# A two-sequence encoder: the sample's second output projection is moved from the kernel's last stage to the end of the stage before

## The chip, the core and the metric

The kernel runs on one core of a Trainium2 chip. The core has a matrix engine (PE, with its weight loads shown apart as PEld), three engines for elementwise work (DVE, ACT, POOL) and a queue that issues DMA transfers (SP, shown as SPq). Each engine works through its own instructions in the order in which they stand. The metric is the device time of one execution in microseconds; lower is better.

## The reference

Two sequences go through the same two-layer encoder with the same weights: the prompt (2048 tokens, called Q or `p` in the kernel) and the sample (1024 tokens, called S or `s`). Width is 1024. One layer is:

```python
xn = rms_norm(h, norm_g)
proj = xn @ w_in
ya = block_attention(qa, ka, va) * silu(a_gate)          # softmax attention over the own tokens
yb = rms_norm(gated_delta_rule(both directions)) * ...   # a scan over chunks of 64 tokens
yc = rms_norm(gla_chunked(both directions)) * ...        # a second, lighter scan
ym = block_attention(m_q, km, vm) * silu(m_gate)         # attention over 256 memory tokens
h = h + concatenate([ya, yb, yc, ym]) @ w_out
```

After two layers `y = rms_norm(h, final_norm_g)`. The mixers `ya`, `yb`, `yc`, `ym` have 4 heads of 64 columns each, so each gives 256 of the 1024 columns that `w_out` reads. All is float32.

## The kernel before

Every projection is a product of 128-wide tiles in which both operands are split into a high and a low part (`whi`, `wlo`, `xhi`, `xlo`); line 280 (`mm3`) issues three matmuls for each of 8 slices of the contraction. An output projection of 512 tokens is 384 such matmuls of 256 columns. Attention (lines 586 to 657) goes by units of one head and 512 query tokens. A unit first takes maxima (line 586, DVE line 587: 16 matmuls for 2048 keys), then for 16 tiles of 128 keys it computes scores (lines 656 and 657), an exponential (`p`, ACT), the product with the values (line 643) and a running sum of `p` on POOL (`acc`, line 155); line 614 sums that over the partitions, and a store to `yT` ends the unit. The prompt's layer has 16 units on memory tokens and then 16 main units; between the 8th and the 9th main unit the keys and values (`kst`, `kh`, `vst`, one buffer each) are loaded anew. The chunk scan (lines 930 to 963, called the scan here) does 32 steps for the prompt, one per 128 tokens and direction. Line 1064 and after are the lighter scan (gla), line 881 the norm of either.

Work is written as streams (Python generators) that `merge` interleaves by estimated costs, and a scheduler then orders each engine's instructions with priorities. One stream, `right`, holds the scans and the sample's mixers through the whole program. Beside it the program runs one stage after the other:

- `projP1`: the prompt's first output projection and second projection (`outproj(Q, 0)`, `proj(Q, 1)`), with the sample's second-layer mixers and the preparation of the prompt's scan in `right`
- slot 3: the prompt's second-layer attention (`mixaP`) and gla (`glaP`) beside what is left in `right`, which is the prompt's scan; it ends when gla and `right` are done
- the last stage: `out_final`, beside what is left of the attention. It goes by blocks of 512 tokens: two of the sample, then four of the prompt. Each block loads the mixers' output (`h<-syT`, `h<-pyT`), splits it, multiplies by four column groups of `w_out`, adds `h` in a tile `ht` and takes the final norm there (`norm_rows`, line 539). Block b of the prompt may start when 10 + 2b main units are done.

The function `outproj`, used for the first layer, goes by blocks of up to 1024 tokens: it adds the residual and stores `h` to DRAM. Projection tiles (pools `xp`, `wp`, `sp`) are freed at the end of a projection stage, and slot 3's tiles take their place.

Of the kernel before, what the change touches and what calls it, by code (L numbers as in the profile page):

```python
# [16 lines left out]
P = 128  # L17
D = 1024
# [5 lines left out]
HB = 3  # L24
# [48 lines left out]
class Kern:  # L73
# [436 lines left out]
    def out_final(self, X, L, hp):  # L510
        nc, I = self.nc, self.I
        g = self.rep(hp, "grep", I["final_norm_g"], D)
        for blk in range(0, X.S, 512):
            n = X.S // 512
            yield from until(lambda: X.mixed >= {("d", L), ("l", L)} and (("a", L) in X.mixed or X.units_done >= 6 * n + 2 * (blk // 512 + 1)))
            xs = self.x_tiles(512)
            ht = self.t(hp, [P, 4, D], "ht", bufs=2)
            self.ld(ht, X.h[blk:blk + 512].rearrange("(j p) c -> p j c", p=P))
            first = self.load_w("wout", (L, 0), 256)()
            yield from self.y_block(X, blk, xs)  # L520

            def sink(c):
                def f(b, ps):
                    v = ht[:, b // P:b // P + 2, c * 256:c * 256 + 256]
                    self.vtt(v, ps, v, ALU.add)
                    if c == 3:
                        for j in (b // P, b // P + 1):
                            self.norm_rows(ht[:, j], g)
                            self.st(X.y[blk + j * P:blk + (j + 1) * P], ht[:, j])
                return f  # L530
            yield from self.groups([("wout", (L, c), 256) for c in range(4)], first, xs, lambda c, w, halves: self.gemm_tok(w, xs, halves, sink(c)))

    def norm_rows(self, h, grep):
        n = h.shape[0]
        junk = self.t(self.sp, [P, D], "gt", mybir.dt.bfloat16)[0:n]
        ss = self.t(self.sp, [P, 1], "ss")[0:n]
        self.act(junk, h, AF.Square, accum_out=ss)
        y = self.rstd(self.sp, ss, 1, 1.0 / D, "xr")
        self.nc.vector.scalar_tensor_tensor(out=h, in0=h, scalar=y, in1=grep, op0=ALU.mult, op1=ALU.mult)
# [578 lines left out]
    def run(self, S, Q):  # L1118
        self.kmT = [self.dram(f"kmT{L}", (256, 512)) for L in range(2)]
        self.vm = [self.dram(f"vm{L}", (512, 256)) for L in range(2)]  # L1120
        go = lambda *streams: merge(self, streams, [right])
        beside = lambda name, *gens: go(Stream(name, chain(*gens)))

        def flow():
            for L in range(2):
                yield from self.gdn(S, L)
                if L:
                    yield from until(lambda: self.slot >= GATE)
                yield from self.gla(S, L, "right", "d")
                yield from self.mixa(S, L, "right", "d")  # L1130
                if L:
                    yield from until(lambda: self.slot >= GATE)
                yield from self.gdn(Q, L)

        def mixes(L):
            return (Stream("mixaP", self.mixa(Q, L, "left", "a")), Stream("glaP", self.gla(Q, L, "left", "l")),
                    Stream("wait", until(lambda: ("d", L) in Q.mixed)))

        right = Stream("right", flow())
        self.slot = 0  # L1140
        self.beside_proj()
        self.open_proj(1024)
        beside("projS0", self.memkv(0), self.memkv(1), self.proj(S, 0))
        beside("projP0", self.proj(Q, 0))
        beside("projS1", self.outproj(S, 0), self.proj(S, 1))
        self.close_proj()
        self.slot = 1
        self.three_mixes()
        go(*mixes(0))
        self.slot = 2  # L1150
        self.beside_proj()
        self.open_proj(1024)
        beside("projP1", self.outproj(Q, 0), self.proj(Q, 1))
        self.close_proj()
        self.slot = 3
        self.three_mixes()
        attn, gla, wait = mixes(1)
        merge(self, [attn, gla, wait], [right], lambda: gla.done and right.done)
        self.beside_out(attn.done)
        self.open_proj(512, "right")  # L1160
        with self.tc.tile_pool(name=self.nm("hp"), bufs=1, side="right") as hp:
            merge(self, [Stream("out", chain(*(self.out_final(X, 1, hp) for X in (S, Q))))], [attn])
        self.close_proj()


# [16 lines left out]
def merge(k, main, side, stop=None):  # L1182
    streams = [*main, *side]
    k.finished.clear()
    for s in streams:
        s.t = 0.0
    stop = stop or (lambda: all(s.done for s in main))
    while not stop():
        live = [s for s in streams if not s.done]
        s = min(live, key=lambda z: z.t)  # L1190
        cost = s.step(k)
        if cost is None:
            s.t = min(o.t for o in live if o is not s) + 500
        else:
            s.t += cost * k.pace.get(s.name, 1)


def until(ready):
    while not ready():
        yield None  # L1200


def chain(*gens):
    for g in gens:
        yield from g
# [65 lines left out]
```

## Time and profile before

| what | value |
|---|---|
| median of 3 runs | 5354.94 us (5354.33 to 5359.36) |
| profiled execution, its own time | 5357.58 us |
| its span, first to last instruction | 5355.5 us |
| PE busy | 4720.6 us, 88% of the span |
| DVE, ACT, POOL busy | 59%, 43%, 35% |
| mean granted clock of PE | 0.941 of full speed |

A busy share of PE is the union of the modelled durations of its matmuls. A window's difference between its length and PE's busy time is called PE's idle time here. Matmuls overlap in the pipeline, so the durations of single rows add up to more than the busy time.

### The profile page before, as it was taken

The numbers are of one execution on the slowest core, as the hardware profiler recorded it, in microseconds if no ns is written. First come the engines' busy times: TensorE is split into PE (matmuls) and PEld (weight loads), VectorE is DVE, ScalarE is ACT, GpSimd is POOL, SyncE is SP. The second block draws the span as 40 slices with busy tenths as digits, with TensorE's granted clock in tenths as the row PEclk, the third lists the DMA queues.
The fourth block names the chain that finished last, engine by engine and source line by source line (L and its number), as shares of the span: only waits on it lengthen the run. The fifth ranks groups of instructions, "written<-read, shape, count | busy, mean of one in ns | idle before, by whom it ended". The sixth has DMA issues, their size and how long they took to land. (4 is left out here: it accounts for less than half of the span.)

```text
span 5355.5 us, 76432 instructions
## 1 busy us (share of the span) xinstructions
PE 4720.6 (88%) x26984; PEld 3644.7 (68%) x26984; DVE 3158.9 (59%) x6175; ACT 2278.8 (43%) x5027; POOL 1864.0 (35%) x1836
## 2 busy tenths in 40 slices
PE   6888999999868887578889889998888989989998
PEld 5777888777757787434455468666777866545887
DVE  4375244454567664588866665636626578877553
ACT  4363233333453534454444432425326365544322
POOL 0141112023332432287656320334215335656212
PEclk8998999999879999789899999999999999999999
DMA  5475353442675743242222246326536542231774
GB/s 192 163 232 182 115 167 120 143 137 94 193 229 179 230 144 91 78 109 58 77 62 70 71 166 216 124 81 187 183 117 200 154 116 79 63 102 42 257 268 151
DMA packets 530118, 755.99 MB, mean 141 GB/s; under 512 B 196096, under 2 KB 389382, under 8 KB 494408
## 3 DMA queue, kind: packets, MB, share of 16 engines
q1 hardware_dynamic: 529736, 751.11, 44.0%
q8 instruction: 214, 3.51, 0.3%
q14 instruction: 168, 1.38, 0.1%
HBM read 490.41 MB, written 260.51 MB: 140 GB/s over the span
## 5 line engine op out<-in xcount | busy, mean ns | idle before, releaser
L280 PE MATMUL b<-whi,xhi 128*128 128x256 f32 x3520 | 1012.2, 288 | 45.7 <-ACT whi L149 13.5
L280 PE MATMUL b<-wlo,xhi 128*128 128x256 f32 x3520 | 1012.0, 288 | 0.5 <-DVE wlo L152 0.5
L280 PE MATMUL b<-whi,xlo 128*128 128x256 f32 x3520 | 1008.0, 288 | 1.1 <-DVE xlo L152 1.1
L155 POOL TENSOR_TENSOR acc<-acc,p 128x512 f32<-128x512 f32 x544 | 741.0, 1362 | 380.0 <-ACT p L146 345.0
L280 PEld LDWEIGHTS b<-whi,xhi 128*128 128x128 f32 x3520 | 681.2, 194 | 75.8 <-ACT xhi L149 24.8
L280 PEld LDWEIGHTS b<-wlo,xhi 128*128 128x128 f32 x3520 | 681.2, 194 | 29.1 <-issue 22.4
L280 PEld LDWEIGHTS b<-whi,xlo 128*128 128x128 f32 x3520 | 679.3, 193 | 30.9 <-issue 22.5
L587 DVE TENSOR_REDUCE mx<-b 128x1 f32<-128x512 f32 (+1 forms) x832 | 502.6, 622 | 322.7 <-PE b L586 318.8
L280 PE MATMUL b<-xhi,whi 128*128 128x512 f32 x1472 | 590.5, 402 | 34.6 <-ACT stg L149 28.8
L146 ACT ACTIVATE p<-b 128x512 f32<-128x512 f32 x736 | 416.9, 595 | 463.2 <-PE b L657 446.0
L280 PE MATMUL b<-xlo,whi 128*128 128x512 f32 x1472 | 588.4, 400 | 0.6 <-DVE xlo L152 0.6
L280 PE MATMUL b<-xhi,wlo 128*128 128x512 f32 x1472 | 587.8, 400 | 0.0
L656 PE MATMUL b<-qh,kst 128*128 128x512 f32 x736 | 344.5, 470 | 41.9 <-DVE mx L587 37.5
L643 PE MATMUL b<-p,vst 128*64 128x512 f32 x1280 | 358.3, 630 | 5.3 <-ACT p L146 4.2
L586 PE MATMUL b<-kst,qh 128*128 128x512 f32 (+1 forms) x832 | 340.2, 436 | 24.6 <-ACT p L146 10.8
L280 PEld LDWEIGHTS b<-xhi,whi 128*128 128x128 f32 x1472 | 276.7, 188 | 114.7 <-ACT stg L149 32.7
L280 PEld LDWEIGHTS b<-xlo,whi 128*128 128x128 f32 x1472 | 276.0, 187 | 73.4 <-issue 9.0
L280 PEld LDWEIGHTS b<-xhi,wlo 128*128 128x128 f32 x1472 | 275.4, 187 | 70.0 <-issue 5.3
L657 PE MATMUL b<-qlm,kh 68*128 68x512 f32 x736 | 297.2, 417 | 14.5 <-DVE qlm L152 14.2
L149 ACT ACTIVATE stg<-b 128x512 f32<-128x512 f32 (+3 forms) x218 | 115.5, 541 | 422.9 <-PE b L280 329.0
L656 PEld LDWEIGHTS b<-qh,kst 128*128 128x128 f32 x736 | 142.3, 194 | 217.6 <-DVE mx L587 104.9
L586 PEld LDWEIGHTS b<-kst,qh 128*128 128x128 f32 x832 | 157.3, 196 | 152.7 <-ACT p L146 49.3
(248 smaller groups left out, 9094.9 us busy)
## 6 DMA issues: line engine op xcount, KB each, us to landing
wlo<-lo_wg SPq DMA_DIRECT2D x48, 1024.0 KB, 7.4
whi<-hi_wg SPq DMA_DIRECT2D x48, 1024.0 KB, 7.2
pcmb<-cm SPq DMA_DIRECT2D x32, 1028.0 KB, 5.5
cm<-pcmb SPq DMA_DIRECT2D x64, 514.0 KB, 3.6
whi<-hi_wout SPq DMA_DIRECT2D x28, 1024.0 KB, 8.5
wlo<-lo_wout SPq DMA_DIRECT2D x28, 1024.0 KB, 6.3
h<-in_wg_dram SPq DMA_DIRECT2D x48, 512.0 KB, 8.2
hi_wg<-whi SPq DMA_DIRECT2D x24, 1024.0 KB, 9.4
```

Source lines behind the costliest of these rows:

```text
L146: self.nc.scalar.activation(out=out, in_=in_, func=func, **k)
L149: self.nc.scalar.activation(out=out, in_=in_, func=AF.Copy)
L155: self.nc.gpsimd.tensor_tensor(out=out, in0=a, in1=b, op=op)
L280: self.nc.tensor.matmul(out=out, lhsT=a, rhs=b, start=(i == 0), stop=(i == len(terms) - 1))
L586: nc.tensor.matmul(out=ps, lhsT=qh[:, qt * P:(qt + 1) * P], rhs=kst[:, lb * LB:(lb + 1) * LB])
L587: nc.vector.tensor_reduce(out=mx[:, qt, lb:lb + 1], in_=ps, axis=AX.X, op=ALU.max)
L643: return nc.tensor.matmul(out=pv[r], lhsT=vst[:, lt, 0:64], rhs=p, start=(lt < 2), stop=(lt >= NL - 2))
L656: nc.tensor.matmul(out=s, lhsT=kst[:, lt * P:(lt + 1) * P], rhs=qh, start=True, stop=False)
L657: nc.tensor.matmul(out=s, lhsT=kh1[0:68, lt * P:(lt + 1) * P], rhs=qlm[0:68], start=False, stop=True)
```

## The change

The sample's second-layer output projection is taken out of the last stage. It now stands behind `proj(Q, 1)` in the stage `projP1`, done by `outproj` as one block of 1024 tokens, which stores `h` to DRAM. A new function `final_norm` follows it: for each of 8 tiles of 128 tokens it loads `h`, takes the norm and stores the result. The last stage keeps the prompt's four blocks.

```diff
+    def final_norm(self, X):
+        g = self.rep(self.sp, "grep", self.I["final_norm_g"], D)
+        for t in range(0, X.S, P):
+            h = self.t(self.sp, [P, D], "h", bufs=HB)
+            self.ld(h, X.h[t:t + P])
+            self.norm_rows(h, g)
+            self.st(X.y[t:t + P], h)
+            yield 1500
...
-        beside("projP1", self.outproj(Q, 0), self.proj(Q, 1))
+        beside("projP1", self.outproj(Q, 0), self.proj(Q, 1), self.outproj(S, 1), self.final_norm(S))
...
-            merge(self, [Stream("out", chain(*(self.out_final(X, 1, hp) for X in (S, Q))))], [attn])
+            merge(self, [Stream("out", self.out_final(Q, 1, hp))], [attn])
```

Lines behind 532 have a number higher by 9 in the changed kernel. The order of instructions is the same on every engine up to the last projection of `projP1`, and differs from there on.

The first place is PE at the end of `projP1`, where the last matmuls of `proj(Q, 1)` stand (`whi_37515` and `wlo_37516` are its last weights). Before, the scan's first steps follow them at once, and shortly behind this piece come the attention's first maxima (L586):

```order
L280 MATMUL b_7255_38224<-whi_37515,xhi_5492_27394 128x256
L280 MATMUL b_7255_38224<-wlo_37516,xhi_5492_27394 128x256
L280 MATMUL b_7255_38224<-whi_37515,xlo_5493_27395 128x256
L938 MATMUL b_7189_37629<-kvi_37608,xtb_7170_37576 128x128 x4
L950 MATMUL b_7191_37639<-ka_37609,wbd_7172_37578 128x128 x4
L962 MATMUL b_7194_37698<-ubd_7174_37580,ka_37609 128x128
L930 MATMUL b_7201_37731<-kvi_37722,xtb_7171_37577 128x128 x4
L963 MATMUL b_7194_37698<-sbd_7176_37582,gq_37638 128x128
L962 MATMUL b_7194_37698<-ubd_7174_37580,ka_37609 128x128
L963 MATMUL b_7194_37698<-sbd_7176_37582,gq_37638 128x128
L934 MATMUL b_7202_37737<-sy_37730,nbd_7181_37587 128x128 x4
```

Now matmuls of the sample's output projection (`whi_38348`, `wlo_38349` are a part of `w_out`) stand there, and the scan's steps between them (L943 is L934 of before):

```order
L280 MATMUL b_7284_38410<-whi_38348,xhi_5490_27392 128x256
L280 MATMUL b_7284_38410<-wlo_38349,xhi_5490_27392 128x256
L943 MATMUL b_7188_37623<-sy_37616,nbd_7180_37586 128x128 x4
L280 MATMUL b_7284_38410<-whi_38348,xlo_5491_27393 128x256
L280 MATMUL b_7284_38410<-whi_38348,xhi_5490_27392 128x256
L280 MATMUL b_7284_38410<-wlo_38349,xhi_5490_27392 128x256
```

768 matmuls of L280 are moved ahead in this way, and 10 of the scan's 32 steps stand among them.

The second place is PE between the 8th and the 9th main unit of the attention, where the keys change: line 614 ends unit 8, line 586 begins unit 9. Before, a step of the scan stands there:

```order
L963 MATMUL b_8419_42239<-sbd_7178_37584,gq_42141 128x128
L614 MATMUL b_9029_44500<-acc_44157,c_ones 64x256
L962 MATMUL b_8420_42247<-ubd_7175_37581,ka_42112 128x128
L963 MATMUL b_8420_42247<-sbd_7179_37585,gq_42141 128x128
L962 MATMUL b_8420_42247<-ubd_7175_37581,ka_42112 128x128
L963 MATMUL b_8420_42247<-sbd_7179_37585,gq_42141 128x128
L586 MATMUL b_9042_44553<-kst_9031_44512,qh_44548 128x512
```

Now only the attention's own instructions stand there (L652 is L643 of before, L623 is L614, L595 is L586):

```order
L652 MATMUL b_9090_45160<-p_45260,vst_8143_42141 64x512
L623 MATMUL b_9126_45276<-acc_45161,c_ones 64x256 x2
L595 MATMUL b_9139_45329<-kst_9128_45288,qh_45324 128x512
L595 MATMUL b_9140_45332<-kst_9128_45288,qh_45324 128x512
L595 MATMUL b_9141_45335<-kst_9128_45288,qh_45324 128x512
```

The scan and gla have ended by then: their last instructions on PE stand at the end of unit 7, where before gla ended at unit 7 and the scan at unit 12 of 16. From unit 8 to most of unit 11 nothing but attention stands on PE; then the prompt's first output block begins. Up to unit 7 the mix is much as before: between the ends of units 1 and 7 stand 8 steps of the scan (before 9), 15 of gla (before 14) and 26 transposed norms (before 24).

The third place is SP at the start of slot 3, where gla's first loads stand (`up`, `bias`, `low`). Before:

```order
L137 DMA pgl<-stg_38273 128x2x256
L137 DMA q_7318_38500<-pmqT 64x512
L137 DMA xtb_7171_37577<-pxt 32x4x32 x4
L137 DMA up_38390<-in_gla_w_gate_up_dram 16x2x128
L137 DMA bias_38392<-in_gla_b_dram 128x2
L137 DMA low_38403<-psmT 16x512
L137 DMA lq_38405<-plqkT 128x512
L137 DMA cm_38006<-pcmb 128x1028
```

Now they stand behind the last store of the new norm pass (`out_dram<-h_40170`):

```order
L137 DMA xtb_7170_37576<-pxt 32x4x32 x4
L137 DMA out_dram<-h_40170 128x1024
L137 DMA q_7765_40910<-pmqT 64x512
L137 DMA cm_39948<-pcmb 128x1028
L137 DMA q_7765_40910<-pmqT 64x512
L137 DMA up_40232<-in_gla_w_gate_up_dram 16x2x128
L137 DMA bias_40234<-in_gla_b_dram 128x2
L137 DMA nbd_7181_37587<-pcmb 32x4x32 x2
L137 DMA low_40245<-psmT 16x512
```

Eight such stores stand in this stretch of SP now and none before, and each waits on SP until its norm is done.

## Rows read from the trace of the kernel before

**Rows 1.** The profile's page: its first line.

```profile
span 5355.5 us, 76432 instructions
```

**Rows 2.** Windows: stretch, its length, busy us (and instructions) by engine, clock, DMA.

```profile
4226.00:4310.00 84.00, 66.92 (x433) 56.26 (x432) 45.61 (x97) 42.56 (x101) 39.06 (x59) 0.92 0.53 142
4310.00:4510.00 200.00, 190.72 (x1057) 130.79 (x1055) 161.42 (x314) 119.50 (x276) 83.14 (x87) 1.00 0.35 99
4510.00:4774.00 264.00, 240.99 (x1192) 141.86 (x1193) 221.17 (x439) 126.84 (x317) 155.62 (x139) 0.98 0.21 61
4774.00:4966.00 192.00, 176.83 (x829) 102.86 (x827) 131.19 (x248) 91.67 (x203) 119.80 (x105) 0.95 0.27 80
4966.00:5245.00 279.00, 277.16 (x1999) 241.13 (x1999) 136.95 (x227) 82.84 (x169) 62.37 (x43) 1.00 0.72 268
5245.00:5355.00 110.00, 87.21 (x615) 76.29 (x613) 32.86 (x65) 27.73 (x62) 19.21 (x15) 0.90 0.37 137
...
4226.00:5355.00 1129.00, 1039.82 (x6115) 749.19 (x6113) 729.21 (x1388) 491.15 (x1126) 479.19 (x448) 0.97 0.41 136
```

**Rows 3.** Groups by line and shape, PE, 4226 to 5355 us: count, busy, mean.

```profile
L280 PE MATMUL b<-whi,xhi 128*128 128x256 f32 x795 | 226.2, 286 | 9.5 <-ACT xhi L149 9.3
```

**Rows 4.** Timeline of PE at 4200 us: start, duration, row.

```profile
4200.10 0.28 PE L280 MATMUL b<-whi,xhi 128*128 128x256 f32 x1
4200.22 0.28 PE L280 MATMUL b<-wlo,xhi 128*128 128x256 f32 x1
```

**Rows 5.** Windows: `outproj(Q, 0)` beside gla; `proj(Q, 1)` beside the scan's preparation.

```profile
3125.00:3275.00 150.00, 149.09 (x1114) 132.67 (x1113) 88.91 (x185) 44.31 (x114) 26.23 (x24) 1.00 0.56 183
3650.00:3800.00 150.00, 121.63 (x624) 102.14 (x625) 95.19 (x180) 81.97 (x167) 69.46 (x74) 0.93 0.59 177
```

**Rows 6.** Waits of PE, 3640 to 3800 us: total, times, longest.

```profile
PE b L805 <- DVE qk L152: 21.8, 4, 7.4
```

**Rows 7.** Timeline of PE, attention's rows: end of unit 7, then between units 8 and 9.

```profile
4774.29 0.65 PE L614 MATMUL b<-acc,c_ones 128*64 128x256 f32 x2
...
4795.43 1.08 PE L643 MATMUL b<-p,vst 128*64 128x512 f32 x4 [0.91 <-ACT p L146]
...
4812.27 0.95 PE L586 MATMUL b<-kst,qh 128*128 128x512 f32 x3
4814.84 0.50 PE L586 MATMUL b<-kst,qh 128*128 128x512 f32 x1 [1.61 <-DVE mx L587]
4816.02 8.32 PE L586 MATMUL b<-kst,qh 128*128 128x512 f32 x12 [0.29 <-DVE mx L587]
4825.07 0.80 PE L656 MATMUL b<-qh,kst 128*128 128x512 f32 x1 [0.31 <-DVE mx L587]
```

**Rows 8.** Window of that gap, all engines.

```profile
4796.00:4825.00 29.00, 21.40 (x68) 12.39 (x64) 24.78 (x49) 10.26 (x26) 9.62 (x9) 0.68 0.45 114
```

**Rows 9.** Timeline of PE at the change from main unit 12 to 13.

```profile
4956.37 0.50 PE L656 MATMUL b<-qh,kst 128*128 128x512 f32 x1 [0.99 <-DVE mx L587]
...
4958.19 0.39 PE L597 MATMUL b<-c_identr,nm 128*4 128x512 f32 x1 [0.32 <-DVE nm L595]
...
4959.68 0.50 PE L657 MATMUL b<-qlm,kh 68*128 68x512 f32 x1 [0.52 <-DVE qlm L152]
```

**Rows 10.** Timeline of PE, end of the first layer's 16th main unit.

```profile
3015.07 1.12 PE L614 MATMUL b<-acc,c_ones 128*64 128x256 f32 x2 [6.26 <-POOL acc L155]
```

**Rows 11.** Timeline before the last output block: SP's store and load, ACT's first split.

```profile
5288.11 0.47 SPq L137 DMA_DIRECT2D pyT<-gt  x1
...
5294.94 1.15 ACT L149 ACTIVATE xhi<-h 128x512 fp32r<-128x512 f32 x2 [7.57 <-DMA h<-pyT]
```

**Rows 12.** Groups of ACT and DVE in the last stage: the final norm's two large passes.

```profile
L146 ACT ACTIVATE gt<-ht 128x1024 bf16<-128x1024 f32 x24 | 25.1, 1048 | 92.4 <-DVE ht L152 92.4
...
L539 DVE SCALAR_TENSOR_TENSOR ht<-ht,xry,grep 128x1024 f32<-128x1024 f32 x24 | 31.3, 1323 | 0.1
```

**Rows 13.** DMA issues of the last stage: KB each, median us from issue to landing.

```profile
out_dram<-ht SPq DMA_DIRECT2D x24, 512.0 KB, 5.7
```

## The prediction

> **What bounds the kernel now.** I read the page's head first: the span is 5355.5 us [rows 1], and the profiled execution took 5357.58 us, 2.1 more than its span and 2.6 more than the median of the runs, 5354.94. The sum below is made against 5357.6; I take the 2.6 off at the end.
>
> The orders agree up to the last projection of `projP1`, which in the trace is at about 4226 us, so only 4226 to 5355 us can change. I cut this tail by windows [rows 2]: the start of slot 3 (4226 to 4310), the memory units and unit 1 (to 4510), units 2 to 7 (to 4774, where the sum of unit 7 stands [rows 7]), units 8 to 12 with the rest of the scan (to 4966), the output blocks beside the last attention (to 5245), and the end. In each the reader should compare the length with PE's busy time. The differences are 17.1, 9.3, 23.0, 15.2, 1.8 and 22.8 us, together 89 of 1129: PE is busy 92% of the tail, and no other engine over 65% of it. DVE comes closest in units 2 to 7, with 221 of 264 us, 84%. So PE bounds the tail, and its idle time is all that there is to win.
>
> **The change part by part.** The change adds no matmul and takes none away. It moves 768 of them (two of six output blocks of 384), at one start every 0.12 us [rows 4] that is 92 us, and it spreads scan and attention anew. The count of rows in the tail shows that this is a third of the output work: 795 of `whi,xhi` [rows 3], and as many of each of the two other kinds, are 2385, six times 384 and a few that still belong to `proj(Q, 1)`. What the same matmuls cost I take as equal at either place, so the time changes by the idle time after, less the 89 of before. I go through it in the new order.
>
> (a) *Sample's output projection with 10 steps of the scan between.* The nearest stretch is `outproj(Q, 0)` beside gla, the same function at full width beside a recurrent mixer: 0.9 us idle in 150 [rows 5]. The other bound is `proj(Q, 1)` beside the scan's preparation: 28.4 us idle in 150 [rows 5], of which 21.8 are four waits for DVE's `qk` [rows 6], a tile that this stretch doesn't make. I take 3, bounds 1 to 28. The splits and stores of `w_out` and the residual's loads move here too; they ran under the matmuls in both places, and without that cover the last block shows the price of one exposed load and split, 6.8 us [rows 11].
>
> (b) *Start of slot 3.* It has 17.1 us idle now. What is new is `final_norm`. A tile takes a load, a square of 1.05 us, small steps, a scaling pass of 1.3 us [rows 12] and a store that lands after 5.7 us [rows 13]; only three `h` buffers turn over. Projection tiles are freed after it, and on SP gla's first loads stand behind its last store. The cover is the scan and the memory units, which stand ahead of gla on PE. The DVE and ACT passes, 8 times 1.3 and 8 times 1.05, come on engines busy 54% and 51% there [rows 2]. I take 22. Lower bound 10, if the scan that is already running fills the start; upper bound 46: the last five tiles in two rounds of about 14.5 us each (load as long as the store, passes, store), 29 us, laid bare.
>
> (c) *Memory units to unit 7.* In the order, units 1 to 7 stand among the same mix of scan, gla and norms as before, at the place where DVE is at 84%. The mix, not the length of the scan, sets the pace of this stretch. Hence I take its 9.3 + 23.0 = 32 idle us again and add 2 for the two norms more, 34; bounds 25 to 50.
>
> (d) *Units 8 to 10 alone.* Here the cover goes. Between units 8 and 9 the new keys are loaded, split and scanned for maxima: from the end of the last product of unit 8 (4795.4 + 1.1) to the first scores of unit 9 at 4825.1 are 28.6 us [rows 7], and only 16 maxima matmuls in it are the attention's (busy 0.95 + 0.50 + 8.32 = 9.8). Now the scan fills the rest, so that PE is busy 21.4 of 29 us [rows 8]. After the change the scan has ended by unit 7, and 28.6 - 9.8 = 19 us stay empty. Each change of unit shows 0.99 + 0.32 + 0.52 = 1.8 us of short waits [rows 9]; with nothing to fill them three cost 5.5. Sum 25, where before units 8 to 12 had 15.2. Bounds 12 (loads and splits come faster without the scan on SP and DVE) to 40.
>
> At this gap PE's granted clock is 0.68 over 29 us [rows 8], so that about two thirds of it lie at 1.2 of the two levels 1.2 and 2.4 GHz, though the scan is at work. The Trainium skill (TensorE: Matmul & The Clock Gate, Part 1) says that an idle array falls to the low level and gets the high one back only after it has been busy again. That speaks against the change, since an emptier gap would send unit 9 off at the low level; if 6 us of its work took 12, the forecast would be 5390. The trace agrees on the fall; no run here shows the emptier gap.
>
> (e) *Four prompt blocks beside units 11 to 16.* Now 1.8 us idle in 279. After, each next block waits for two more units, so three times some 67 attention rows stand alone between matmuls of blocks. They cover the store to `yT`, the load and the split of a new block. I take 6, three ends of unit at 1.8; bounds 2 to 25 (three times the 6.8 of rows 11).
>
> (f) *The end.* 22.8 now: the wait for unit 16, its store, the load and the split, then the norm behind the last matmul. Unit 16 now has matmuls of the third prompt block between its last tiles; after the change its last six tiles stand alone. Its sum then waits for POOL, as at the end of the first layer, 6.3 us [rows 10]. I take 28, bounds 23 to 35.
>
> Sum: 3 + 22 + 34 + 25 + 6 + 28 = 118, less 89 gives +29 us: 5357.6 + 29 - 2.6 = 5384 us. In words: the scan goes under a projection that was already dense, and the output blocks that could have filled the attention's gaps are spent when the gaps come.
>
> **The rivals.** *The idle time only moves.* The keys' gap shortens and the start hides in the scan: 1 + 17 + 30 + 18 + 4 + 24 = 94, +5, 5360 us. For it speaks that PE's busy time is conserved; against it, that the scan must be gone from the gap.
>
> *Slot 3 shrinks by the scan (faster).* If it is the scan's serial chain, and not the mix, that paces slot 3, taking 10 of 32 steps out shortens it with its idle time: (9.3 + 23.0 + 15.2) x 22/32 = 33 for (c) and (d) together, 10 for the start, 3 + 4 + 23 for the others: 73, -16, 5339 us. For it: 84 us of slot 3's start have 17 idle while the scan alone runs. Against it: PE is 91% and DVE 84% busy in units 2 to 7. It decides for faster once (c) and (d) together fall under 38.
>
> *PE waits for the scan among the projection's matmuls.* (a) at 28, the others as summed: 143, +54, 5409 us. Against it, 0.9 idle beside gla.
>
> *The norm pass holds slot 3 back.* (b) at 46: 142, +53, 5408 us. Against it, the scan and 16 memory units stand ready.
>
> **How the numbers follow.** A change of 0.2%, 10.7 us, is about what a measurement of this kernel can tell from none; so faster is under 5344, slower over 5366. My forecast holds 0.45, with a range of its own of 5366 to 5408; the moved idle time 0.20; the shrunk slot 0.15; the two waits 0.10 each. Slower has 0.45 + 0.20 = 0.65, same 0.20, faster 0.15. The range reaches down to 5342, which leaves about two thirds of the faster case out, and up to 5420, past both waits, for two bounds that meet: 0.8 within.
>
> **What would show it.** In the profile after: `L280` rows and scan rows mixed from 4226 to about 4380 with PE near 100%; unit 7 ending later than now by the 92 us moved ahead, 10 us of idle time and the last quarter of the scan; then about 19 us of empty PE beside 16 maxima matmuls, with no scan row; the first prompt block only in unit 11; units 11 to 16 beside 1536 projection matmuls; and a span near 5387. The forecast is wrong if PE's idle time behind unit 7 is under 45 us (25 + 6 + 28 = 59 is expected) or that before it under 48 (3 + 22 + 34 = 59); if the start of slot 3 has over 35 us idle, the norm pass is the cause.

## The result, and the profile after

| what | before | after |
|---|---|---|
| median | 5354.64 us (4 runs, 5349.59 to 5359.36) | 5402.05 us (4 runs, 5401.57 to 5402.85) |
| ratio | 1 | 1.0089, 95% interval 1.0071 to 1.0106 |
| span of the profiled execution | 5355.5 us | 5401.1 us |

The changed kernel is slower by about 47 us, where 29 were forecast. The windows of its tail follow, cut at the places of the terms (a) to (f): the sample's projection, the start of slot 3, the rest of it to the end of unit 7, units 8 to 10 alone, the blocks beside the attention, the end. The columns are those of [rows 2].

```profile
4226.00:4380.00 154.00, 150.64 (x1271) 149.95 (x1271) 50.09 (x95) 48.94 (x113) 34.55 (x58) 0.99 0.64 207
4380.00:4460.00 80.00, 61.10 (x390) 53.81 (x388) 50.59 (x126) 44.09 (x115) 22.32 (x37) 0.89 0.68 202
4460.00:4936.00 476.00, 431.23 (x2148) 263.86 (x2149) 408.30 (x821) 246.83 (x599) 236.00 (x218) 0.98 0.29 85
4936.00:5046.00 110.00, 92.28 (x281) 37.39 (x279) 56.00 (x84) 43.36 (x80) 65.13 (x50) 0.85 0.25 79
5046.00:5305.00 259.00, 247.06 (x1494) 181.04 (x1492) 132.71 (x196) 79.51 (x158) 102.87 (x75) 0.99 0.41 151
5305.00:5401.00 96.00, 73.74 (x514) 63.59 (x514) 32.86 (x61) 24.08 (x56) 17.03 (x13) 0.88 0.37 140
4226.00:5401.00 1175.00, 1056.05 (x6090) 749.65 (x6089) 730.54 (x1381) 486.81 (x1118) 477.91 (x448) 0.96 0.39 127
```

The length less PE's busy time gives the idle time of each term:

| term | forecast | measured |
|---|---|---|
| (a) sample's projection | 3 | 3.4 |
| (b) start of slot 3 | 22 | 18.9 |
| (c) to the end of unit 7 | 34 | 44.8 |
| (d) units 8 to 10 alone | 25 | 17.7 |
| (e) blocks beside units 11 to 16 | 6 | 11.9 |
| (f) end | 28 | 22.3 |
| sum | 118 | 119.0 |

The idle time is what was forecast, 119 against 118. But PE's busy time in the tail, which the forecast kept, grew from 1039.8 us [rows 2] to 1056.1: 16 us more, with the same matmuls. 30 + 16 are the 46 us between the spans. Much of the 16 goes with the clock: PE's busy time at the low level, 1.2 GHz, is 76.7 us in this tail and was 46.1 in the one before. At that level L280 starts come 0.21 us apart (5 in 1.06 us behind 4236.25), at the high one 0.12 [rows 4], so the 30.6 us more would be about 17 at the high level; by this estimate 13 of the 16 us are the clock's. What they cost in time isn't shown by that.

Between units 8 and 9 PE's timeline now shows the attention alone, in place of [rows 7]:

```profile
4957.21 1.08 PE L652 MATMUL b<-p,vst 128*64 128x512 f32 x4 [1.82 <-ACT p L146]
4965.01 1.11 PE L623 MATMUL b<-acc,c_ones 128*64 128x256 f32 x2 [6.72 <-POOL acc L155]
...
4971.82 7.37 PE L595 MATMUL b<-kst,qh 128*128 128x512 f32 x12 [0.41 <-DVE mx L596]
4979.59 1.40 PE L665 MATMUL b<-qh,kst 128*128 128x512 f32 x2 [0.40 <-DVE mx L596]
...
4984.32 0.63 PE L666 MATMUL b<-qlm,kh 68*128 68x512 f32 x1
...
4988.90 0.39 PE L666 MATMUL b<-qlm,kh 68*128 68x512 f32 x1
```

No scan row is left. The gap from the end of the last product to the first scores is 21.3 us, not 28.6: the keys come sooner. The missing scan alone doesn't explain that. In the run `a_short` below no step stands there either, and the gap is 25.4 us; its last stage's loads (`ht<-ph`) are issued only 7 us ahead of the keys' loads, here 15.5, and the split of the new keys begins 9.0 us behind the issue of the keys' loads, here 2.9. The wait for POOL's sum, 6.72 us, is that of [rows 10], now with nothing beside it. The clock falls at 4961.4, while PE waits for POOL (rows of 0.63 us, of 0.39 again from 4988.9 on).

For the experiments the tail is cut at events, since executions differ by some 10 us in what lies ahead of it: at SP's last store of `plqkT` (shortly before the end of `proj(Q, 1)`), the last L280 before slot 3, the stores to `yT` of the 16th memory unit and of main units 7, 10, 12 and 16. Length of each stretch in us, in brackets the steps of the scan in it (256 rows of L950, or of its line in another kernel, are 32 steps):

| kernel | to slot 3 | memory units | units 1 to 7 | 8 to 10 | 11, 12 | 13 to 16 | end | all |
|---|---|---|---|---|---|---|---|---|
| before | 49.0 (0) | 203.5 (12) | 335.8 (12) | 118.5 (6) | 68.2 (2) | 322.6 | 67.4 | 1165 |
| after | 199.4 (10) | 226.1 (12) | 326.8 (10) | 103.7 (0) | 101.1 (0) | 189.9 | 66.5 | 1214 |
| scan held | 149.9 (0) | 182.7 (10) | 355.7 (14) | 128.7 (4) | 69.7 (4) | 242.8 | 66.4 | 1196 |
| pass at head of last stage | 199.8 (10) | 199.1 (11) | 338.4 (11) | 116.6 (0) | 101.0 (0) | 191.0 | 66.5 | 1213 |
| pass between blocks | 201.9 (10) | 195.3 (11) | 339.1 (11) | 111.6 (0) | 104.0 (0) | 200.5 | 67.0 | 1219 |
| 10 steps out of slot 3 | 200.6 (10) | 216.6 (12) | 289.8 (0) | 107.6 (0) | 101.2 (0) | 191.2 | 66.2 | 1173 |
| same 10 out, scan held | 149.4 (0) | 189.9 (9) | 335.1 (11) | 116.3 (2) | 101.2 (0) | 190.7 | 66.3 | 1149 |

A prompt block beside units 11 and 12 is 384 matmuls, 46 us at 0.12; the moved part is 92.

### The profile page after: what moved, and what is told of

Same layout as the page of the kernel before. It is cut to its first block, busy times and chain, and to the rows that moved or that the text cites. A ratio compares the mean times of both kernels' runs of the same rounds, so it can differ in the third digit from the quotient of the medians.

```text
span 5401.1 us, 76502 instructions
## 1 busy us (share of the span) xinstructions
PE 4739.9 (88%) x26984; PEld 3651.5 (68%) x26984; DVE 3167.7 (59%) x6175; ACT 2278.2 (42%) x5027; POOL 1860.2 (34%) x1836
## 5 line engine op out<-in xcount | busy, mean ns | idle before, releaser
L280 PE MATMUL b<-whi,xhi 128*128 128x256 f32 x3520 | 1014.5, 289 | 45.0 <-ACT whi L149 12.6
L280 PE MATMUL b<-wlo,xhi 128*128 128x256 f32 x3520 | 1013.3, 288 | 1.2 <-DVE wlo L152 1.2
L280 PE MATMUL b<-whi,xlo 128*128 128x256 f32 x3520 | 1010.2, 288 | 1.1 <-DVE xlo L152 1.1
L280 PEld LDWEIGHTS b<-whi,xhi 128*128 128x128 f32 x3520 | 681.3, 194 | 71.9 <-ACT xhi L149 25.7
L280 PEld LDWEIGHTS b<-whi,xlo 128*128 128x128 f32 x3520 | 679.9, 194 | 34.6 <-issue 26.2
L280 PEld LDWEIGHTS b<-wlo,xhi 128*128 128x128 f32 x3520 | 681.5, 194 | 29.9 <-issue 22.5
L280 PE MATMUL b<-xhi,whi 128*128 128x512 f32 x1472 | 589.6, 401 | 32.0 <-ACT stg L149 26.3
L280 PE MATMUL b<-xlo,whi 128*128 128x512 f32 x1472 | 587.7, 399 | 0.6 <-DVE xlo L152 0.6
L280 PE MATMUL b<-xhi,wlo 128*128 128x512 f32 x1472 | 587.3, 399 | 0.0
L652 PE MATMUL b<-p,vst 128*64 128x512 f32 x1280 | 362.4, 637 | 6.9 <-ACT p L146 6.2
L595 PE MATMUL b<-kst,qh 128*128 128x512 f32 (+1 forms) x832 | 339.2, 439 | 28.5 <-ACT p L146 12.3
L280 PEld LDWEIGHTS b<-xhi,whi 128*128 128x128 f32 x1472 | 276.3, 188 | 111.9 <-ACT stg L149 30.4
L280 PEld LDWEIGHTS b<-xlo,whi 128*128 128x128 f32 x1472 | 275.7, 187 | 73.4 <-issue 9.0
L280 PEld LDWEIGHTS b<-xhi,wlo 128*128 128x128 f32 x1472 | 275.2, 187 | 70.0 <-issue 5.3
L666 PE MATMUL b<-qlm,kh 68*128 68x512 f32 x736 | 299.1, 419 | 15.6 <-DVE qlm L152 15.4
L595 PEld LDWEIGHTS b<-kst,qh 128*128 128x128 f32 x832 | 158.1, 197 | 169.8 <-ACT p L146 58.8
```

Source lines behind the costliest of these rows:

```text
L280: self.nc.tensor.matmul(out=out, lhsT=a, rhs=b, start=(i == 0), stop=(i == len(terms) - 1))
L595: nc.tensor.matmul(out=ps, lhsT=qh[:, qt * P:(qt + 1) * P], rhs=kst[:, lb * LB:(lb + 1) * LB])
L652: return nc.tensor.matmul(out=pv[r], lhsT=vst[:, lt, 0:64], rhs=p, start=(lt < 2), stop=(lt >= NL - 2))
L666: nc.tensor.matmul(out=s, lhsT=kh1[0:68, lt * P:(lt + 1) * P], rhs=qlm[0:68], start=False, stop=True)
```

## The experiments

Each ratio is taken against runs of the kernel before on the same chip; 0.1% is 5.4 us. The medians of that kernel there are 5349 to 5366 us, so an expected time is compared by the ratio.

**Scan held back to slot 3** (`hold_scan`).

```diff
+            if L and X.S > 1024:
+                yield from until(lambda: self.slot >= 3)
             yield from self.gdn_scan(X, pp)
```

> The changed kernel, but the prompt's scan may not begin before slot 3, so that none of its steps stands among the sample's projection matmuls and all 32 steps are left for slot 3. Theory A (the loss comes from spent cover: the scan runs under a projection that needs no filler and is missing beside the attention): slot 3 gets back the mix that it has in the kernel before, the last stage has four blocks to fill units 13 to 16, and of the 46 us most is given back: 5354 to 5370 us, PE idle in the tail about 89 to 105 us. Theory B (the norm pass and the loads at the start of slot 3 cost it, or the two functions in place of one): nothing of that is touched, 5390 to 5405 us.

Measured: 1.0060 (1.0044 to 1.0077), 5394 us, where the kernel before takes 5361. About 15 of the 47 us come back, though the intervals still touch (1.0077 here, 1.0071 there). It is much less than theory A asks for and, at 5387 us by the ratio, a little more than B allows. The projection takes 50 us less, but PE now has 8.4 us of idle time up to slot 3 (3.4 in the changed kernel). The edit doesn't keep the whole scan out: the preparation of its first step still stands at the start of the block, and there PE waits for a copy on ACT, which stands behind a split that waits for a load of the block:

```profile
4258.77 1.15 ACT L149 ACTIVATE xhi<-h 128x512 fp32r<-128x512 f32 x2 [6.91 <-DMA h<-syT]
4259.83 0.58 ACT L149 ACTIVATE sy<-b 128x512 f32<-128x512 f32 x1
4260.46 2.08 PE L943 MATMUL b<-sy,nbd 128*128 128x128 f32 x8 [8.00 <-ACT sy L149]
```

At the start of slot 3 the norm pass stands as in the changed kernel, but other work stands beside it: the first memory unit is stored 32 us into slot 3, behind two steps of the scan, in the changed kernel 95 us, behind eight, and in the kernel before 71 us, behind six. From there to the end of unit 7 the table has 538.4 us with 24 steps, and 539.3 with 24 in the kernel before, which has no pass. In this mix the pass costs nothing that the sums show.

**Norm pass at the head of the last stage** (`norm_last`).

```diff
-        beside("projP1", ..., self.outproj(S, 1), self.final_norm(S))
+        beside("projP1", ..., self.outproj(S, 1))
...
+            g = self.rep(hp, "grep", self.I["final_norm_g"], D)
-            merge(self, [Stream("out", self.out_final(Q, 1, hp))], [attn])
+            merge(self, [Stream("out", chain(self.final_norm(S, g), self.out_final(Q, 1, hp, g)))], [attn])
```

> The changed kernel, but the sample's norm pass stands at the start of the last stage, ahead of the prompt's first block, and no longer at the start of slot 3. Theory A (spent cover): the start of slot 3 has 18.9 us of PE idle with the pass and had 17.1 in the kernel before, so that little can be won: 5393 to 5404 us. Theory B (the pass holds slot 3 back): a gain of 15 us or more, 5387 us or less.

Measured: 1.0084 (1.0069 to 1.0099): no gain, as theory A has it. But the table shows that this is a sum of two: from the start of slot 3 to the end of unit 7 it is 15.4 us shorter (the first memory unit is stored after 70 us, not 95), units 8 to 10 are 12.9 longer. The pass now lies where the keys change, as the window of this kernel at that place shows:

```profile
4957.00:4985.00 28.00, 20.62 (x38) 9.44 (x38) 21.28 (x42) 10.20 (x25) 2.67 (x2) 0.50 0.96 323
```

The 16 DMA engines are 96% busy there, and 38 matmuls stand in 28 us.

**Half of the move** (`half`): the sample's first 512 tokens behind the prompt's projection, the other 512 in the last stage.

```diff
-        beside("projP1", ..., self.outproj(S, 1), self.final_norm(S))
+        beside("projP1", ..., self.outproj(S, 1, 512), self.final_norm(S))
...
-            merge(self, [Stream("out", self.out_final(Q, 1, hp))], [attn])
+            merge(self, [Stream("out", chain(self.out_final(S, 1, hp, 512), self.out_final(Q, 1, hp)))], [attn])
```

> Only the sample's first block of 512 tokens is moved behind the prompt's second projection (with its norm pass); its second block stays in the last stage, ahead of the prompt's. Theory A (spent cover, in proportion): about 5 steps of the scan are spent under the moved block, the scan reaches to unit 9 or 10, a block is left for the units behind, and about half of the 46 us is lost: 5370 to 5385 us. Theory B (a fixed cost of the norm pass or of the second function): nearly the whole loss stays, 5390 us or more. Theory C (only the bare gap between units 8 and 9 counts, and half the move leaves it filled): 5355 to 5365 us.

Measured: 1.0084 (1.0067 to 1.0101). Half the move costs as much as all of it, the time of theory B, so the loss isn't in proportion to the moved work or to the steps spent (here 4 under the projection). Its last stage begins within unit 10 with the sample's block; the prompt's first follows at the end of that unit, and each later one waits for its pair of units as in the changed kernel.

**Blocks in another order, in the kernel before** (`s_behind`).

```diff
-        for blk in range(0, X.S, 512):
+        for X, blk in seq:   # (Q, 0), (Q, 512), (S, 0), (Q, 1024), (S, 512), (Q, 1536)
```

> The kernel before, with one edit: the last stage takes its six blocks in another order, two of the prompt, one of the sample, the third of the prompt, the other of the sample, the last of the prompt. Theory A (blocks that wait for nothing are worth most where the attention has gaps): the sample's second block lies over the end of unit 16, where PE has 22.8 us idle now; 8 to 15 us are won, 5340 to 5347 us. Theory B (the end is set by the last unit's sum, store, load and split whatever lies before it): within 5 us of before.

Measured: 0.9997 (0.9988 to 1.0006): theory B. 992 in place of 384 matmuls of L280 lie behind the store of unit 16, and it is worth nothing that can be measured.

**Attention ahead of the output blocks** (`b_attn_first`, `a_attn_first`, `hold_attn_first`: the kernel before, the changed one, the one with the scan held).

```diff
-LE = {"right": 1000, "mixS1": 500}
+LE = {"right": 1000, "mixS1": 500, "mixaP": 1500}
```

> The kernel before, with one number added: in the last stage the attention's instructions get a priority 1500 ahead of the output blocks, so that unit 16 ends while 1177 of the last stage's matmuls of L280 are still to come (384 in the kernel before). Theory A (what costs in the last stage is that dense output matmuls go ahead of the attention and are spent when its end must be waited for): PE's idle time there falls from 25 us to 8 to 15, 5337 to 5347 us. Theory B (attention beside which less dense work stands costs as much in its own waits as it saves at the end): 5350 us or more.

> The changed kernel with the same number added. The prompt's blocks still have to wait for their pairs of units, so that at the end of unit 16 only 470 matmuls of L280 are left instead of 384. Theory A (as for the run beside it, but here the waits for pairs of units bind, since no block is ready ahead of time): a gain of 5 to 12 us, 5389 to 5397 us, and the distance to the kernel before with the same number grows over 46 us. Theory C (the loss of the change is made in slot 3 and not in the last stage): the same gain as the run beside it, so that the distance stays at 46 us.

> The changed kernel with the scan held back to slot 3 and the same number added. Here the last stage begins at unit 12, two of the prompt's blocks are ready, and 903 matmuls of L280 are left at the end of unit 16. Theory A: the end is covered, 15 us or more are won against the run with the scan held back alone (5394 us), 5370 to 5380 us. Theory B: nothing is won.

Measured: 1.0010 (1.0000 to 1.0020), 1.0072 (1.0058 to 1.0086), 1.0042 (1.0026 to 1.0057). The kernel before gains nothing. The changed kernel comes 9 us nearer, which the intervals leave uncertain. In its profile units 13 to 16 take 178.5 us in place of 189.9, but 46 matmuls more are left for the end; from unit 11 to the end it is 345.6 us against 357.5. With the number in both kernels the distance is 33 us (5389.6 against 5356.9), where theory A had it grow over 46 and theory C had it stay. With the scan held as well 25 of the 47 us are back. Theory A's prices fail for the kernel before; where blocks have to wait for units, the order counts for some 10 us.

**Norm pass between the prompt's first two blocks** (`norm_mid`), and **all three edits together** (`all_three`).

```diff
+            merge(self, [Stream("out", chain(self.out_final(Q, 1, hp, g, 0, 512), self.final_norm(S, g), self.out_final(Q, 1, hp, g, 512, 2048)))], [attn])
```

> The changed kernel, but the sample's norm pass stands in the last stage between the prompt's first and second output block, where PE has dense matmuls to do. With the pass at the head of the last stage the memory units were done 14 us sooner after the projection, and the 12 us came back as idle time where the keys change. Theory B (the pass costs 10 to 14 us wherever DVE and ACT are waited for, and nothing beside dense matmuls): 5388 to 5395 us. Theory A (the pass costs nothing of its own; spent cover is all): 5398 to 5408 us, as with the pass at the head of the last stage.

> The changed kernel with all three edits: the scan held back to slot 3, the attention ahead of the output blocks in the last stage, and the norm pass between the prompt's first two blocks. The sample's projection block itself stays where the change puts it. If the three losses are separate ones and these are all: the 5372 us of the first two edits less what the norm pass is worth (10 to 14 us), 5356 to 5364 us, within the 0.2% of the kernel before. If the block at its new place costs something by itself: 5368 us or more.

Measured: 1.0101 (1.0080 to 1.0121) and 1.0097 (1.0082 to 1.0113). Both forecasts of mine fail. Between the blocks the pass isn't free: the table has `norm_mid` 18 us shorter to the end of unit 7 and 22 us longer behind it, and with the pass there the two good edits lose 30 us. (The 14 us that the expectation gives the memory units are 27 in the table, with one step less.) The wait list of PE and the window of `all_three` show where:

```profile
PE b L280 <- ACT xhi L149: 40.3, 1, 40.3
```

```profile
5204.00:5244.00 40.00, 1.04 (x4) 0.19 (x2) 18.37 (x48) 15.80 (x41) 0.00 (x0) 0.55 0.82 286
```

And SP's timeline there (two of the loads of the pass, and behind them the first load of the next block):

```profile
5217.33 0.33 SPq L137 DMA_DIRECT2D h<-sh  x1
...
5239.97 0.33 SPq L137 DMA_DIRECT2D h<-sh  x1
5241.19 0.38 SPq L137 DMA_DIRECT2D h<-pyT  x1
```

The output block loads the mixers' output into the same three `h` buffers. So the next block's first load waits until the pass gives a buffer back, and the attention, which had been put ahead, has nothing left to fill PE. In these 40 us PE has 1 us of work. The rival on the norm pass had priced five bare tiles at 29 us; eight cost 40 here. In the changed kernel the pass isn't bare in this way.

**Matmuls that compute nothing, where the keys change** (`warm`): `dummies(ins, n)` puts n products of the identity with itself behind `ins` on PE, into a bank that nobody reads.

```diff
+            if u == 7 and SL > 1024:
+                dummies(last[0].ins, 40)
...
+                    if u == 8:
+                        dummies(mm.ins, 2)
```

> The changed kernel with matmuls that compute nothing added where the keys change: 40 behind the last product of unit 8 and 2 behind each of the 16 maxima matmuls of unit 9. Theory D (a part of the loss is the matmuls that run at half the clock after the empty gap, 76.7 us of busy time at half clock in the tail where the kernel before has 46.1): the gap from 4961 to 4989 us keeps the full clock, the maxima and the first rows of unit 9 take 0.40 us again for 0.63, and 3 to 7 us are won although PE has 72 matmuls more: 5393 to 5399 us. Theory A alone (the clock is of no weight here, only the waits): the same time or up to 5 us more.

Measured: 1.0097 (1.0079 to 1.0115). The window of the gap here, that of the changed kernel, and PE's rows here:

```profile
4974.00:4999.00 25.00, 23.92 (x99) 16.97 (x95) 18.68 (x28) 5.72 (x10) 7.17 (x5) 1.00 0.37 95
```

```profile
4955.00:4980.00 25.00, 13.92 (x27) 5.63 (x25) 19.46 (x29) 7.59 (x15) 9.65 (x7) 0.63 0.37 107
```

```profile
4973.49 1.08 PE L663 MATMUL b<-p,vst 128*64 128x512 f32 x4 [1.82 <-ACT p L146]
4974.50 9.40 PE L583 MATMUL b<-c_identr 128*128 128x512 f32 x40
...
4997.31 0.98 PE L677 MATMUL b<-qh,kst 128*128 128x512 f32 x2
...
5000.98 0.40 PE L678 MATMUL b<-qlm,kh 68*128 68x512 f32 x1
```

The clock is at its full level, 1.00, the rows of unit 9 take 0.40 us again, and in sum nothing is won: units 8 to 10 take 104.8 us against 103.7. But this sum has a gain in it. From its first scores to its store unit 9 takes 32.9 us (4997.31 to 5030.18) against 35.7 (4979.59 to 5015.32; three more runs at the low level there have 35.7 to 36.1), so the low level had cost 2.9 us there. From the last product of unit 8 to the first scores it is 23.8 us, start to start, against 22.4, with the added matmuls between the maxima. The other 2.5 us are lost in units 8 and 10, where the clock in this execution is at the low level for 3.0 and 3.4 us, in the changed kernel's for 1.0 and none. Theory D's gain for the whole doesn't come; what the clock alone is worth, without the cost of matmuls that keep it up, this run can't say.

**Ten steps of the scan left out, at the one place or the other** (`a_short`, `hold_short`).

```diff
+            short = X.S > 1024 and self.slot >= 2
             for s in range(NT):
+                if short and 3 <= s < 8:
+                    continue
                 a = prep(0, s, 2 * s)
```

> The changed kernel with 10 of the 32 steps of the prompt's second-layer scan left out (chunks 3 to 7 of either direction, so a part of the output is not computed; all norms and stores are kept). 10 steps go on under the sample's projection as now, and 12 in place of 22 are left for slot 3. Theory E (in slot 3 a step of the scan rides along: a unit of the attention alone took 29 us, as long as with scan steps beside it, so that steps taken out of slot 3 shorten it by little; under a projection a step costs its whole time on PE): 8 to 20 us less than the changed kernel, 5382 to 5394 us. Theory F (work on PE costs the same at either place, as the prediction had it): 10 steps of 5.3 us, 45 to 55 us less, 5347 to 5357 us.

> The same 10 steps left out, and the scan held back to slot 3: no step stands under the sample's projection, and slot 3 has 22 steps, as in the changed kernel. So against the changed kernel it is 10 steps less under the projection. Theory E: the stretch of the projection falls from 199 us after the last store of the keys' part to about 145, and nothing is given back: 45 to 58 us less than the changed kernel, 5344 to 5357 us, 30 to 45 us under the run beside it. Theory F: the same as the run beside it within 10 us.

Measured: 1.0011 (0.9998 to 1.0024) and 0.9970 (0.9959 to 0.9980). Against the changed kernel's 1.0089 that is 0.78%, 42 us, for ten steps out of slot 3, and 1.19%, 64 us, for ten steps out of the projection. Theory E in its strong form falls: a step in slot 3 isn't free. But the places differ by 22 us, over twice the 10 that F allows. By stretches: without its 10 steps the projection is 50 us shorter in the table's last row (5.0 each; with the scan held 7.5 us of this row are again a wait of L943, so a step is worth more than that); units 1 to 7 without theirs are 37 shorter (3.7 each). In the kernel before, units 8 to 12 had 8 steps and took 186.7 us; after, without a step, 204.8 less the block's 46, which is 159: 28 us for 8 steps, 3.5 each. These prices make some 13 of the 22 us. The memory units add to it: they take 189.9 us with 9 steps against 216.6 with 12, some 16 us beyond the steps, part of which units 1 to 10 take back. With the scan held the norm pass stands beside memory units there, as in `hold_scan`.

Why a step is cheaper there, two windows show in part, one of the attention without the scan, from the changed kernel, and one with it, from the kernel before:

```profile
5015.00:5044.00 29.00, 26.13 (x89) 10.83 (x89) 16.23 (x26) 11.22 (x22) 19.48 (x15) 1.00 0.06 19
```

```profile
4867.00:4897.00 30.00, 28.80 (x153) 17.56 (x152) 19.91 (x42) 15.95 (x35) 21.17 (x19) 1.00 0.19 50
```

The first holds 89 matmuls, all of the attention; the second holds 73 of the attention and 80 of the scan and its norm. At the first window's rate the 73 take 23.8 us, so 6.2 of the 30 go to the 80, which are 1.7 steps of 48: 3.7 us a step, an estimate. Of PE's busy time the 73 have 21.4 us by that rate, so the 80 have 7.4, or 4.4 us a step. Under the projection a step has 5.4: 195.6 us busy with ten steps, 141.7 with the scan held. So about 1 us of a step is saved because lengths overlap, since matmuls of the attention alone lie apart and each is counted with more of its own length, and about 0.7 us fills time in which PE was idle. The Trainium skill (TensorE: Matmul & The Clock Gate, Part 2, Step-by-step: what each phase is for) says that an isolated matmul can't hide its drain and one in a stream can. This case's rows agree, by the profile's modelled ends: in the attention rows of 0.40 us start 0.23 us apart (4991.42 and 4991.65 in the changed kernel).

## Why the prediction was right in sign and short in size

- **The sign and the idle time** held: PE's idle time behind unit 7 is 17.7 + 11.9 + 22.3 = 51.9 us and before it 67.1, both past the marks of 45 and 48 under which the forecast would have been wrong. The scan ends with unit 7, the first block begins in unit 11, no scan row stands in the gap. That the sum fits to 1 us is luck: (c) and (e) came out 10.8 and 5.9 us over, (b), (d) and (f) 3.1, 7.3 and 5.7 under.
- **The step that failed** is "What the same matmuls cost I take as equal at either place, so the time changes by the idle time after, less the 89 of before". Busy time of PE is no constant of the work: 16 us are missing by it, about 13 of them by the clock's level, which the prediction priced at one gap alone. By lengths, ten steps of the scan and the block's start lengthened the projection by 199.4 - 49.0 - 92 = 58 us. Taken away from units 8 to 12, 8 of them gave 28 back; the other two were taken from units 1 to 7, which are 9 shorter. These 21 us have the size of what the experiments with ten steps left out (22 us) and with the scan held (15 us) show. Of the rest of the 49 us in the table's last column, 23 lie in the memory units, with as many steps as before and the norm pass new, and 5 in units 13 to 16, beyond the 1152 matmuls that are gone from there.
- **(a)**, 3 against 3.4: right about waits, but it counted a step under the projection as paid for by one less in slot 3.
- **(b) and (c)** together 56 against 63.7. (c) was undersized: "the mix, not the length of the scan" was to give the old idle time again. By lengths, the memory units and units 1 to 7 took 552.9 us with 22 steps, where before 539.3 had 24. Moving the pass away took 15 to 18 us off this stretch, and put 13 to 22 elsewhere. (b) counted on "the scan and the memory units" as cover. But eight steps of the scan ran before the first memory unit was stored, 95 us into slot 3 and 24.5 later than in the kernel before. With the scan held the memory units do come first, and the pass costs nothing there. Under the sample's projection, with the rows still on chip, it was not tried.
- **(d)**, 25 against 17.7: the lower side held, the keys came sooner, though not by the missing scan alone (`a_short`). **The clock** there fell as the prediction said: 0.85 in units 8 to 10. The Trainium skill (TensorE: Matmul & The Clock Gate, Part 1) says that an idle array falls to the low level, and the trace agrees: it fell in the 6.7 us in which PE waited for POOL. Of the 6 us that I gave for it 2.9 are there, in unit 9, but the run that kept the clock up lost more than that around it.
- **(e) and (f)**: 11.9 for 6 and 22.3 for 28. The longest wait for POOL's sum behind 5066 us is 2.2 us, not the 6.3 that (f) took from [rows 10].
- **The rivals.** That slot 3 shrinks by the scan and makes it faster was wrong, though ten steps out of it do shorten it, by 42 us: they cost more where they went. The bare norm pass exists, but in `all_three`.

**Open**: with scan held and attention first, 22 us (1.0042) remain, 16 in the profiled executions' tails. By its stretches about 7 lie in the projection, where PE again waits 6.8 us for the first step's preparation, and 8 in units 8 to 10, with two steps less than before; which of the new order's waits make the 8 isn't settled. Nor is it why half the move costs as much as the whole: in its trace PE is busy at the low level for 97.2 us, more than in any other run that does all of the work, but no run shows that as the reason. The prices by stretches come from one execution of each kernel. No version here that does all of the work beats the kernel before.

## What to carry to other kernels

Work that rides between the matmuls of a latency-bound stretch costs less there (here 3.5 to 3.7 us a step in place of 5 to 6) than beside dense work, so don't let a side stream run ahead under a projection that needs no filler. Sum lengths of stretches with and without the moved work, and not PE's busy time, which grows when the clock falls and when matmuls lie apart. A separate pass over rows that were normed in place before takes loads, buffers and two engines; what that costs depends on what PE has to do beside it (here nothing beside the memory units, 40 us bare). Look at which buffers it shares with the next stage's loads.

## What was not expected of the hardware

A low granted clock can cost far less than half of the time that it lasts. It was at the low level for 27 us through the change of keys (0.63 over 25 us, 4955 to 4980), and unit 9 lost 2.9 us by it. The 72 matmuls that kept the clock at 1.00 gave these back and took 1.4 us in the gap, and in all units 8 to 10 took 104.8 us against 103.7. And 80 matmuls of the scan among 73 of the attention took 7.4 us of PE's busy time by the rate of the attention alone, where under a projection they would have had 9.
